# Other places in SBUF for the matmul operands of a two-layer encoder: weight buffers 32 bytes further apart each, x and three other tiles shifted

## The chip, the core and the metric

The kernel runs on one core of one Trainium2 chip. The metric is the device time of one execution in microseconds; the profile is one execution taken by the hardware profiler. SBUF is the on-chip memory that the engines work in: 128 partitions, and a tile lies at the same byte offset in each of them. "Place" below means that offset. TensorE (PE) multiplies a stationary operand of 128 columns (the weight load, PEld) with a moving operand that streams by, 256 or 512 columns here; both come from SBUF, and the sum goes to PSUM, in banks of 512 fp32 columns.

## The reference

A sequence of 512 positions by 1024 features passes two layers and a last norm. Layer 0 mixes positions by stick-breaking attention (16 heads of 64, causal), layer 1 by an RG-LRU block (projections, a causal convolution of four taps, gates per block, a linear recurrence). Each mixer is followed by an MLP of width 4096 with squared ReLU.

```python
def reference(x, ...):
    for layer in range(2):
        h = rms_norm(x, norm_mix[layer])
        y = stick_breaking_attention(h, w_qkv, w_o) if layer == 0 else rglru_block(h, ...)
        x = x + y
        h = rms_norm(x, norm_mlp[layer])
        x = x + jnp.square(jax.nn.relu(h @ mlp_w1[layer])) @ mlp_w2[layer]
    return rms_norm(x, norm_final)
```

All data are float32. The kernel keeps that precision with three products for one: each operand is split in a high half (rounded to the type fp32r, which TensorE takes in one pass) and a low half (the rest), and high by high, high by low and low by high are added up.

## The kernel before, in words

Features lie on partitions in 8 chunks of 128, positions along a partition. The normed x stands in `xgh` (high) and `xgl` (low), 8 chunks of 512 columns each; `bh` and `bl` (blocks, high and low) are of the same size and hold the mixer's output, and in an MLP the squared activations of its first half; `sh` and `sl` hold those of the second half.

Every weight tile of 128 by 1024 elements (4 KiB a partition) comes by DMA into a `raw` buffer (three of them). ScalarE (ACT) rounds it into `wh`, VectorE (DVE) writes the rest into `wl`, four buffers of each, and TensorE reads them. This goes round robin, so that each step's weights lie in the next of the four buffers. Where the layers need it, two further buffers of `wh` and `wl` stand in a pool of their own (`wmore`).

Three loops make nearly all of the matmuls:

- `dense` and `three` (L217 to L231): weights stationary, x or a block moving, 512 columns; for each of 8 chunks the triple `wh` by high, `wl` by high, `wh` by low. It does the q and k products, the output products of both mixers, the first quarter of the MLP, the RG-LRU projections.
- `v_steps` (L478 to L480): x stationary, weights moving, 256 columns.
- In the MLP a scheme with 7 products in place of 8 (blocks of a matrix are added ahead of the multiplication). `up` (L966) multiplies with weights stationary and 256 columns moving: chunks of `xgh` and `xgl`, or sums of chunks, whose high halves stand in `s41` (and in the last chunk of `bh`, `bl`) and whose low halves stand in eight tiles `low`. `times` (L1061) has the activations stationary (`bh`, `bl`, `sh`, `sl`) and the weights moving, 512 columns.

TensorE's order is written out by the code (it is scheduled by hand); in the MLP and the RG-LRU part the order on ACT and DVE is fixed too (class `Ordered`, the string `ORDER`). PE takes one instruction after the other; weights for the next matmul are loaded beside the one that runs.

The places follow from the order in which the pools and tiles are opened. Tiles of one pool stand one behind the other and each begins at a multiple of 32 bytes. In the kernel before nearly all operands are whole numbers of 512 bytes long, and everything that lies between them is a few small tiles. So all four buffers of `wh` and of `wl` begin at the same offset in a 512-byte grid. The table gives the places as the built program has them, taken modulo 512, in the two kernels:

| operand | before | after |
|---|---|---|
| `xgh`, `xgl` in attention and the RG-LRU part | 32 | 128 |
| `xgh`, `xgl` in both MLPs | 32 | 256 |
| `bh`, `bl` | 32 | 256 |
| the four `wh`, and `wl` of the same step | 288, 288, 288, 288 | 256, 288, 320, 352 |
| two more `wh`, `wl` in the RG-LRU part | 480 | 96 |
| `sh`, `sl` (second half of the activations) | 480 in layer 0, 96 in layer 1 | 128 |
| `s41` | 480 in layer 0, 96 in layer 1 | 96 |
| `low`, 8 tiles | 480 (one of them 96 in layer 1) | 96 |
| q, k, v halves, transposed weights of attention | 480 | 96 |

A chunk of x is 2048 bytes and a column block of weights 512, so a chunk's or block's own place in the 512-byte grid is that of its tile.

Of the kernel before, what the change touches and what calls it, by code (L numbers as in the profile page):

```python
# [24 lines left out]
EPS = 1e-6  # L25
RG_C = 8.0
SCALE = HD ** -0.5


START = [  # L30
# [31 lines left out]
def hybrid_encoder(  # L62
# [55 lines left out]
    V.memset(eps_t, EPS)  # L118
# [22 lines left out]
    class Squares:  # L141


        def __init__(self):
            self.acc = work.tile([P, S], F32, tag="ssq", name="ssq", bufs=1)
            self.begun = False
# [16 lines left out]
        def inv_squares(self, ps):  # L163

            for t in range(S // P):
                PE.matmul(
                    ps[:, t : t + 1], self.acc[:, t * P : (t + 1) * P], ones[:, 0:1],
                    start=True, stop=True,
                )
            n = S // P  # L170
            rr = work.tile([P, 2 * n], F32, tag="rr", name="rr", bufs=1)
            V.tensor_scalar(rr[:, :n], ps[:, :n], 1.0 / D, EPS, ALU.mult, ALU.add)
            V.reciprocal(rr[:, :n], rr[:, :n])
            V.tensor_scalar(rr[:, n:], rr[:, :n], -1.0, None, ALU.mult)
            return rr


    def slab_parts(src, cuts):

        raw = wpool.tile([P, C, P], F32, tag="raw", name="raw", bufs=3)  # L180
        wh = wpool.tile([P, C, P], F32R, tag="wh", name="wh")
        wl = wpool.tile([P, C, P], F32R, tag="wl", name="wl")
# [12 lines left out]

        return wh, wl, fetch, part
# [5 lines left out]
    def slab(src, cut=1, ks=range(C)):  # L202
        raws = rawpools[next(loads) % len(rawpools)]
        raw = raws.tile([P, C, P], F32, tag="raw", name="raw", bufs=3 if raws is wpool else 1)
        k = slice(ks.start, ks.stop)
        nc.sync.dma_start(out=raw[:, k, :], in_=src[:, k, :])
        pool = wpools[next(slabs) % len(wpools)]
        wh = pool.tile([P, C, P], F32R, tag="wh", name="wh")
        wl = pool.tile([P, C, P], F32R, tag="wl", name="wl")
        for i in range(cut):  # L210
            k = slice(ks.start + i * len(ks) // cut, ks.start + (i + 1) * len(ks) // cut)
            A.copy(wh[:, k, :], raw[:, k, :])  # L212
# [18 lines left out]
    def beside(ws, ah, al, pss, at, ks=range(C)):  # L231
# [7 lines left out]

    ctx.enter_context(tc.manual_schedule(engines={mybir.EngineType.PE}))  # L240


    lams = {
        n: const.tile([P, C], F32, tag=f"lam_{n}", name=n)
        for n in ("ab", "pp", "den", "s1", "s2", "pl", "c8", "c4")
    }
    c8, c4 = lams["c8"], lams["c4"]

    def softplus():

# [28 lines left out]
    NB = S // P  # L279
    PAIRS = H // 2  # L280
    half = [slice(0, HD), slice(HD, P)]
    so, early = {}, {}
# [7 lines left out]
    with ExitStack() as actx:  # L290
        hp = actx.enter_context(tc.tile_pool(name="hp", bufs=2))
        sp = actx.enter_context(tc.tile_pool(name="sp", bufs=1))


        later = sp.tile([P, S], F32, tag="later", name="later")
        G.memset(later, 0.0)
        G.affine_select(
# [11 lines left out]
        for i in range(2):  # L309
            both = []  # L310
            for nm in ("h", "l"):
                t = sp.tile([P, 2 * P], F32R, tag=f"last{nm}{i}", name=f"last{nm}{i}")
                G.memset(f(t[:, :P]), 0.0)
                both.append(t)
            lasts.append(both)
# [117 lines left out]
        def inverse():  # L433
# [333 lines left out]
    class Mlp:  # L767
# [28 lines left out]
        def __init__(self, ctx, layer):  # L796
            self.layer, self.sq, self.first = layer, Squares(), None
            self.V, self.A = Ordered(V), Ordered(A)
            self.mp = ctx.enter_context(tc.tile_pool(name=f"mlp{layer}", bufs=2))
            self.c = [  # L800
                self.mp.tile([P, 2, S], F32, tag=f"c{i}", name=f"c{i}", bufs=1) for i in range(4)
            ]
            self.begun, self.a = set(), {}
            self.turns = count()
            self.blocks = ExitStack()
            self.bp = self.blocks.enter_context(tc.tile_pool(name=f"blocks{layer}", bufs=2))
            self.u, self.lows, self.s3, self.slots = {}, {}, [], None

            self.s41 = self.bp.tile([P, C // 2, S], F32R, tag="s41", name="s41", bufs=1)

        def y(self, t, h):

# [207 lines left out]

        def operand(self, raw):
            pool = wpools[next(slabs) % len(wpools)]
            wh = pool.tile([P, C, P], F32R, tag="wh", name="wh")
            wl = pool.tile([P, C, P], F32R, tag="wl", name="wl")
# [288 lines left out]
    with ExitStack() as mctx:  # L1313
        mlp = Mlp(mctx, 0)
# [4 lines left out]
        last = {}  # L1319
# [57 lines left out]
    with ExitStack() as rctx:  # L1377
# [48 lines left out]

        def weights_high(key):
            pool = wmore if next(made) % 6 > 3 else wpool
            wh = pool.tile([P, C, P], F32R, tag="wh", name="wh")
            wl = pool.tile([P, C, P], F32R, tag="wl", name="wl")  # L1430
            ws[key] = wh, wl
            OA.copy(wh, raws[key])

# [140 lines left out]
        for k in range(C):  # L1574
            for c in range(4):
                ps, wh, wl = begun[c]
                three(ps, bh[:, k, :], bl[:, k, :], wh[:, k, :], wl[:, k, :], k == 0, k == C - 1)

    residual(w_ro, "mlp1", begun, {4: ws["o4"]})
    wctx.close()  # L1580


    with ExitStack() as mctx:
        lp = mctx.enter_context(tc.tile_pool(name="last", bufs=1))
        mlp = Mlp(mctx, 1)

        def between(c):
# [20 lines left out]
                )  # L1608


        A.activation(lp.tile([P, 1], F32, tag="rt", name="early"), eps_t, AF.Sqrt)

        ss = lp.tile([P, NB, 3], F32, tag="ss", name="ss")
        bias = lp.tile([P, NB], F32, tag="bias", name="bias")

        def square(t, h, i, cols=slice(0, S), end=False):

# [129 lines left out]
```

## Time and profile before

| | |
|---|---|
| median of 2 runs | 1048.83 us (1048.66 to 1049.0) |
| the profiled execution, span from the first to the last instruction | 1047.9 us |
| PE busy | 1035.1 us, 99% of the span, 5868 matmul records |
| DVE, ACT, POOL busy | 863.1, 701.5, 179.2 us |
| DMA | 159.41 MB, mean 152 GB/s |

The profile counts a span of 1047.9 us; the run's time is 0.9 us more than it. The end of a matmul is modelled in this profile, and matmuls are pipelined: one that is shown with 0.39 us starts 0.23 us ahead of the next. How long a matmul holds the engine is therefore read from the distance of two starts in the timeline, not from its own duration. For that a stretch is taken in which nothing but matmuls of one kind follow each other: the start of the last minus the start of the first, by the number between.

### The profile page before, as it was taken

Reading aid. Unit: us, or ns where it says so; the run is one execution under the profiler, and the core shown is the slowest. Engines: PE = TensorE matmul, PEld = TensorE weight load, DVE = VectorE, ACT = ScalarE, POOL = GpSimd, SP = SyncE. Lnnn points to the kernel's source line nnn. Section 1 sums busy time; section 2 is a strip of 40 time slices with the busy share of each in tenths; the row PEclk is TensorE's granted clock in tenths of the full one; section 3 lists DMA queues with packets and bytes.
Section 4 is the critical chain, followed back from the end, with each engine's and each line's share of the span. In section 5 each row is a group of like instructions: output and inputs, shape, how many; then the busy total and the mean of one; then the engine's idle time right before and its main releaser. Section 6 shows DMA issues by size and latency. Waiting matters only on the chain.

```text
span 1047.9 us, 15859 instructions
## 1 busy us (share of the span) xinstructions
PE 1035.1 (99%) x5868; PEld 902.8 (86%) x5868; DVE 863.1 (82%) x1147; ACT 701.5 (67%) x1082; POOL 179.2 (17%) x238
## 2 busy tenths in 40 slices
PE   8999999999999999999999999999999999999997
PEld 7888888888888988988988788888888988988986
DVE  7888787848788898898899799984789797897897
ACT  6767676836766773773775699964755773773775
POOL 2344344420000010010011121200000010010013
PEclk9999999999999999999999999999999999999999
DMA  6745354537536667567582483352345667567553
GB/s 225 204 137 141 101 149 104 153 109 274 149 80 190 181 139 204 165 140 207 164 208 81 109 214 112 91 221 93 88 86 173 174 142 206 158 139 204 145 125 101
DMA packets 52828, 159.41 MB, mean 152 GB/s; under 512 B 6672, under 2 KB 7952, under 8 KB 52752
## 3 DMA queue, kind: packets, MB, share of 16 engines
q1 hardware_dynamic: 41808, 120.13, 34.4%
q0 software_dynamic: 10368, 37.75, 20.9%
q8 instruction: 46, 0.75, 0.3%
q10 hardware_dynamic: 576, 0.52, 0.2%
q14 instruction: 30, 0.25, 0.1%
HBM read 137.41 MB, written 4.19 MB: 135 GB/s over the span
## 4 chain that ended last, share of the span: by engine, by line
PE 88%; DVE 5%; ACT 3%; issue 2%; DMA 2%; ACTq 0%; POOL 0%; DVEq 0%; POOLq 0%
PE ps_t L1061 14%; PE ps_acc L966 8%; PE ps_z L966 8%; PE ps_acc L1061 7%; PE ps_acc L219 5%; PE ps_acc L221 5%; PE ps_acc L220 5%; PE ps_o L966 5%; PE ps_z L1061 4%; PE ps_o L219 2%; PE ps_t L220 2%; PE ps_o L220 2%; PE ps_o L221 2%; PE ps_t L221 2%; PE ps_t L219 2%
## 5 line engine op out<-in xcount | busy, mean ns | idle before, releaser
L757 ACT CAST wh<-b 128x1024 fp32r<-128x1024 f32 x168 | 174.0, 1047 | 125.6 <-DVE b L757 76.7
L757 DVE TENSOR_TENSOR wl<-b,wh 128x1024 fp32r<-128x1024 f32 x168 | 203.8, 1221 | 50.5 <-ACT wh L757 50.1
L1043 POOL DMA_DIRECT2D b<-in_w_dn x40 | 35.0, 875 | 360.9 <-DVE b L757 204.6
L219 PE MATMUL ps_acc<-xgh,wh 128*128 128x512 f32 x192 | 78.5, 409 | 0.0
L221 PE MATMUL ps_acc<-xgl,wh 128*128 128x512 f32 x192 | 75.2, 392 | 0.0
L220 PE MATMUL ps_acc<-xgh,wl 128*128 128x512 f32 x192 | 75.1, 391 | 0.0
L581 DVE TENSOR_TENSOR_SCAN scan<-keep,later 128x128 f32<-128x128 f32 (+1 forms) x64 | 59.6, 933 | 18.8 <-ACT keep L571 10.9
L214 DVE TENSOR_TENSOR wl<-raw,wh 128x512 fp32r<-128x512 f32 (+2 forms) x70 | 60.9, 895 | 16.2 <-ACT wh L212 16.1
L757 ACT ACTIVATE u<-u 128x512 f32<-128x512 f32 x100 | 63.1, 632 | 6.5 <-DVE u L757 4.8
L212 ACT CAST wh<-raw 128x512 fp32r<-128x512 f32 (+2 forms) x70 | 50.8, 759 | 23.1 <-PE ps_acc L221 7.3
L1043 POOL DMA_DIRECT2D b<-in_w_up x24 | 20.8, 867 | 240.5 <-DVE b L757 72.1
L585 POOL TENSOR_TENSOR w<-w,scan 128x128 f32<-128x128 f32 (+1 forms) x64 | 51.9, 813 | 55.9 <-DVE scan L581 53.2
L757 DVE TENSOR_TENSOR b<-b,b 128x1024 f32<-128x1024 f32 x48 | 58.7, 1224 | 1.3
L757 DVE TENSOR_TENSOR u<-u 128x512 f32<-128x512 f32 (+1 forms) x92 | 54.9, 596 | 2.7 <-ACT u L757 1.1
L966 PE MATMUL ps_z<-xgh,wh 128*128 128x256 f32 x192 | 54.2, 282 | 0.0
L966 PE MATMUL ps_z<-xgh,wl 128*128 128x256 f32 x192 | 54.1, 282 | 0.0
L757 ACT CAST wh<-raw 128x1024 fp32r<-128x1024 f32 x46 | 47.9, 1045 | 9.3 <-PE ps_acc L1061 8.4
L966 PE MATMUL ps_acc<-low,wh 128*128 128x256 f32 x192 | 53.6, 279 | 0.0
L1061 PE MATMUL ps_t<-wl,sh 128*128 128x512 f32 x126 | 50.1, 398 | 0.0
L1061 PE MATMUL ps_t<-wh,sh 128*128 128x512 f32 x126 | 49.6, 394 | 0.0
L1061 PE MATMUL ps_t<-wh,sl 128*128 128x512 f32 x126 | 49.4, 392 | 0.0
L1061 PE MATMUL ps_t<-wh,bh 128*128 128x512 f32 x126 | 49.2, 391 | 0.0
(399 smaller groups left out, 3434.4 us busy)
## 6 DMA issues: line engine op xcount, KB each, us to landing
b<-in_w_dn SPq DMA_DIRECT2D x48, 512.0 KB, 4.5
b<-in_w_dn POOLq DMA_DIRECT2D x40, 512.0 KB, 5.5
b<-in_w_up SPq DMA_DIRECT2D x36, 512.0 KB, 4.6
b<-in_w_up POOLq DMA_DIRECT2D x24, 512.0 KB, 5.3
raw<-in_w_m SPq DMA_DIRECT2D x16, 512.0 KB, 4.1
raw<-in_w_dn SPq DMA_DIRECT2D x16, 512.0 KB, 4.7
raw<-in_w_in SPq DMA_DIRECT2D x16, 512.0 KB, 4.2
raw<-in_w_qk SPq DMA_DIRECT2D x12, 512.0 KB, 3.7
```

Source lines behind the costliest of these rows:

```text
L212: A.copy(wh[:, k, :], raw[:, k, :])
L214: V.tensor_tensor(wl[:, k, :], raw[:, k, :], f(wh[:, k, :]), ALU.subtract)
L219: PE.matmul(ps, wh, ah, start=start, stop=False)
L220: PE.matmul(ps, wl, ah, start=False, stop=False)
L221: PE.matmul(ps, wh, al, start=False, stop=stop)
L581: V.tensor_tensor_scan(sc[:, S - n : S][:, ::-1], keep[:, :n][:, ::-1], later[:, S - n :][:, ::-1], 1.0, ALU.mult, ALU.max,)
L585: G.tensor_tensor(wt, wt, sc[:, S - n + 1 : S + 1], ALU.mult)
L757: ins = getattr(self.e, name)(*args, **kwargs)
L966: PE.matmul(ps[:, i * HS : (i + 1) * HS], m, y, start=new and i == k == n == 0, stop=i == 1 and k == C // 2 - 1 and n == 2, skip_group_che ...
L1043: G.dma_start(out=unit[b].rearrange("p j n -> p (j n)"), in_=unit["src"](to), accum_op=ALU.add)
L1061: PE.matmul(ps, m, y[:, jj, cols], start=first and n == 0, stop=last and n == 2, skip_group_check=not new,)
```

## The change

Nothing is computed otherwise. The instructions of every engine stand in the same order as before, with the same shapes; one of them (a one-column square root that loads ACT's table early, at the start of the second MLP) writes into an unused column of another tile. What changes are the places:

- `wh` and `wl` come from pools of their own, each buffer 8 elements (32 bytes) longer than its data; `colt` (the columns of scales, 384 bytes) lies between the two pools, so that `wh` and `wl` of one step lie at the same offset in the 512-byte grid.
- `xgh` and `xgl` have 32 elements (128 bytes) of room more. `x_at` says at which end of it x lies: at 0 in attention and in the RG-LRU part, 128 bytes further in both MLPs.
- `s41` is 32 bytes longer, so that `sh` and `sl` and the raw blocks behind it move by 32 bytes against it; small tiles (`lams`, `ss`, `bias`, the `last` tiles) are opened elsewhere, and `rr` is 64 bytes in place of 32.

```diff
+ASIDE = 32
+APART = 8
+STEP = 8
+LINE = 16
...
     wpool = ctx.enter_context(tc.tile_pool(name="wpool", bufs=4))
+    halfpools = {}
+    halfpools["wh"] = ctx.enter_context(tc.tile_pool(name="whpool", bufs=4))
+    mid = ctx.enter_context(tc.tile_pool(name="mid", bufs=1))
+    halfpools["wl"] = ctx.enter_context(tc.tile_pool(name="wlpool", bufs=4))
...
-    colt = const.tile([P, cols.shape[1]], F32, tag="colt", name="colt")
+    colt = mid.tile([P, cols.shape[1]], F32, tag="colt", name="colt")
...
-    xgh = const.tile([P, C, S], F32R, tag="xgh", name="xgh")
-    xgl = const.tile([P, C, S], F32R, tag="xgl", name="xgl")
+    xgh_t = const.tile([P, C * S + ASIDE], F32R, tag="xgh", name="xgh")
...
+    xgl_t = const.tile([P, C * S + ASIDE], F32R, tag="xgl", name="xgl")
+    xgh = xgl = None
+
+    def x_at(aside):
+
+        nonlocal xgh, xgl
+        xgh, xgl = (
+            t[:, aside : aside + C * S].rearrange("p (c s) -> p c s", s=S) for t in (xgh_t, xgl_t)
+        )
+
+    x_at(0)
...
-            rr = work.tile([P, 2 * n], F32, tag="rr", name="rr", bufs=1)
+            rr = work.tile([P, LINE], F32, tag="rr", name="rr", bufs=1)
...
+    def weights(pool, tag):
+
+        step = STEP * (pool is wpool)
+        pool = halfpools[tag] if step else pool
+        t = pool.tile([P, C * P + step], F32R, tag=tag, name=tag)
+        return t[:, : C * P].rearrange("p (k f) -> p k f", f=P)
...
-        wh = pool.tile([P, C, P], F32R, tag="wh", name="wh")
-        wl = pool.tile([P, C, P], F32R, tag="wl", name="wl")
+        wh = weights(pool, "wh")
+        wl = weights(pool, "wl")
...
+    x_at(ASIDE)
     residual(w_so, "mlp0", so, so_next)
...
-            self.s41 = self.bp.tile([P, C // 2, S], F32R, tag="s41", name="s41", bufs=1)
+            t = self.bp.tile([P, C // 2 * S + APART], F32R, tag="s41", name="s41", bufs=1)
+            self.s41 = t[:, : C // 2 * S].rearrange("p (k s) -> p k s", s=S)
...
         def end(ws, xs):
+            x_at(0)
             for i in range(2):
...
+    x_at(ASIDE)
     residual(w_ro, "mlp1", begun, {4: ws["o4"]})
...
-        lp = mctx.enter_context(tc.tile_pool(name="last", bufs=1))
         mlp = Mlp(mctx, 1)
...
-        A.activation(lp.tile([P, 1], F32, tag="rt", name="early"), eps_t, AF.Sqrt)
+        A.activation(mlp.c[0][:, 0, :1], eps_t, AF.Sqrt)
```

More of the change, by code (lines that the diff above doesn't have):

```diff
@@ L116, in hybrid_encoder @@
     make_identity(nc, ident)
+    xgh_t = const.tile([P, C * S + ASIDE], F32R, tag="xgh", name="xgh")
     eps_t = const.tile([P, 1], F32, tag="eps", name="eps_t")
     V.memset(eps_t, EPS)
-    xgh = const.tile([P, C, S], F32R, tag="xgh", name="xgh")
-    xgl = const.tile([P, C, S], F32R, tag="xgl", name="xgl")
+    bias = const.tile([P, S // P], F32, tag="bias", name="bias")
+    ss = const.tile([P, S // P, 3], F32, tag="ss", name="ss")
+    lams = {
+        n: const.tile([P, C], F32, tag=f"lam_{n}", name=n)
+        for n in ("ab", "pp", "den", "s1", "s2", "pl", "c8", "c4")
+    }
+    c8, c4 = lams["c8"], lams["c4"]
+    xgl_t = const.tile([P, C * S + ASIDE], F32R, tag="xgl", name="xgl")
[6 more added lines that the diff above has]
+    x_at(0)
     bh = const.tile([P, C, S], F32R, tag="bh", name="bh")
@@ L170, in inv_squares @@
             n = S // P
-            rr = work.tile([P, 2 * n], F32, tag="rr", name="rr", bufs=1)
+            rr = work.tile([P, LINE], F32, tag="rr", name="rr", bufs=1)
             V.tensor_scalar(rr[:, :n], ps[:, :n], 1.0 / D, EPS, ALU.mult, ALU.add)
             V.reciprocal(rr[:, :n], rr[:, :n])
-            V.tensor_scalar(rr[:, n:], rr[:, :n], -1.0, None, ALU.mult)
+            V.tensor_scalar(rr[:, n : 2 * n], rr[:, :n], -1.0, None, ALU.mult)
             return rr
+    def weights(pool, tag):
[3 more added lines that the diff above has]
+        return t[:, : C * P].rearrange("p (k f) -> p k f", f=P)
     def slab_parts(src, cuts):
         raw = wpool.tile([P, C, P], F32, tag="raw", name="raw", bufs=3)
-        wh = wpool.tile([P, C, P], F32R, tag="wh", name="wh")
-        wl = wpool.tile([P, C, P], F32R, tag="wl", name="wl")
+        wh = weights(wpool, "wh")
+        wl = weights(wpool, "wl")
         def fetch(i, queue=nc.sync):
@@ L240, in hybrid_encoder @@
     ctx.enter_context(tc.manual_schedule(engines={mybir.EngineType.PE}))
[L243 to L247, printed above, removed]
     def softplus():
@@ L292, in hybrid_encoder @@
         sp = actx.enter_context(tc.tile_pool(name="sp", bufs=1))
+        last_of = {
+            (nm, i): sp.tile([P, 2 * P], F32R, tag=f"last{nm}{i}", name=f"last{nm}{i}")
+            for i in range(2) for nm in "hl"
+        }
         later = sp.tile([P, S], F32, tag="later", name="later")
@@ L311, in hybrid_encoder @@
             for nm in ("h", "l"):
-                t = sp.tile([P, 2 * P], F32R, tag=f"last{nm}{i}", name=f"last{nm}{i}")
+                t = last_of[nm, i]
                 G.memset(f(t[:, :P]), 0.0)
@@ L1022, in operand @@
             pool = wpools[next(slabs) % len(wpools)]
-            wh = pool.tile([P, C, P], F32R, tag="wh", name="wh")
-            wl = pool.tile([P, C, P], F32R, tag="wl", name="wl")
+            wh = weights(pool, "wh")
+            wl = weights(pool, "wl")
             wh, wl = (t.rearrange("p (j k) f -> p j (k f)", j=2) for t in (wh, wl))
@@ L1428, in weights_high @@
             pool = wmore if next(made) % 6 > 3 else wpool
-            wh = pool.tile([P, C, P], F32R, tag="wh", name="wh")
-            wl = pool.tile([P, C, P], F32R, tag="wl", name="wl")
+            wh = weights(pool, "wh")
+            wl = weights(pool, "wl")
             ws[key] = wh, wl
@@ L1608, in factors @@
                 )
-        A.activation(lp.tile([P, 1], F32, tag="rt", name="early"), eps_t, AF.Sqrt)
-        ss = lp.tile([P, NB, 3], F32, tag="ss", name="ss")
-        bias = lp.tile([P, NB], F32, tag="bias", name="bias")
+        A.activation(mlp.c[0][:, 0, :1], eps_t, AF.Sqrt)
         def square(t, h, i, cols=slice(0, S), end=False):
```

## The prediction

> **What bounds the kernel now.** I read the page first, then who waits on PE, then busy time by stage, then the timeline of PE in stretches of one kind. The page:
>
> ```profile
> span 1047.9 us, 15859 instructions
> PE 1035.1 (99%) x5868; PEld 902.8 (86%) x5868; DVE 863.1 (82%) x1147; ACT 701.5 (67%) x1082; POOL 179.2 (17%) x238
> ...
> PEclk9999999999999999999999999999999999999999
> ...
> PE 88%; DVE 5%; ACT 3%; issue 2%; DMA 2%; ACTq 0%; POOL 0%; DVEq 0%; POOLq 0%
> ```
>
> PE is busy in 99% of the span, at a granted clock of 0.9 or more in every slice, and holds 88% of the chain that ended last. A busy PE need not be a PE at its peak, so the next question is whether it waits. The view of waits on PE, longest first:
>
> ```profile
> PE ps_z L437 <- DVE ssq L422: 1.6, 1, 1.6
> PE ps_z L381 <- DVE eps_t L118: 1.1, 1, 1.1
> PE ps_z L966 <- ACT u L757: 1.0, 1, 1.0
> PE ps_t L220 <- DVE wl L757: 0.8, 1, 0.8
> ```
>
> These are the four longest, 4.5 us of 1047.9 together. No engine and no DMA can give more than that back. What is left is the pace of the matmuls themselves. The busy time by stage, for one MLP stretch of each layer, says who would be next:
>
> ```profile
> core 0: us, PE busy (x) PEld busy (x) DVE busy (x) ACT busy (x) POOL busy (x), PEclk, DMA share, GB/s
> 290.00:460.00 170.00, 170.00 (x1071) 153.39 (x1071) 147.41 (x193) 116.37 (x153) 16.50 (x19) 1.00 0.63 160
> 764.00:920.00 156.00, 154.97 (x984) 139.74 (x983) 134.98 (x152) 99.23 (x127) 13.89 (x16) 1.00 0.62 162
> ```
>
> DVE has 147.41 of 170 us (87%) and 134.98 of 156 us (87%). A PE that is 2 to 4% faster still does not catch up with DVE's sum. The pace of PE, in the timeline: of each stretch the first row and the row that follows its last.
>
> ```profile
> 439.53 0.28 PE L966 MATMUL ps_o<-s,wh 128*128 128x256 f32 x1
> ...
> 442.25 0.28 PE L966 MATMUL ps_z<-xgh,wh 128*128 128x256 f32 x1
> ...
> 447.94 0.28 PE L966 MATMUL ps_z<-xgh,wh 128*128 128x256 f32 x1
> ...
> 450.82 0.40 PE L1061 MATMUL ps_t<-wh,bh 128*128 128x512 f32 x1
> ...
> 805.67 0.28 PE L966 MATMUL ps_acc<-s,wh 128*128 128x256 f32 x1
> ...
> 808.50 0.39 PE L966 MATMUL ps_acc<-bh,wh 128*128 128x256 f32 x1
> ```
>
> Each of the three stretches is one half product of `up`: 24 matmuls of the same shape, no wait between. The first takes 2.72 us, 113.3 ns each; it streams `s41` and `low` of layer 0, which lie at 480 in the 512-byte grid, past weights at 288. The second takes 2.88 us, 120.0 ns each; it streams x, at 32, past the same weights. The third is the first one's product in layer 1, where `s41` and one `low` lie at 96: 2.83 us, 117.9 ns. Only places differ. With 512 columns:
>
> ```profile
> 294.86 0.39 PE L1061 MATMUL ps_t<-wh,bh 128*128 128x512 f32 x1
> ...
> 300.30 0.39 PE L1061 MATMUL ps_t<-wh,sh 128*128 128x512 f32 x1
> ...
> 302.82 0.39 PE L1061 MATMUL ps_t<-wh,sl 128*128 128x512 f32 x1
> ...
> 769.24 0.40 PE L1061 MATMUL ps_t<-wh,sh 128*128 128x512 f32 x1
> ...
> 772.04 0.40 PE L1061 MATMUL ps_z<-wh,bh 128*128 128x512 f32 x1
> ```
>
> From 294.86 to 300.30 lie 24 matmuls with `bh` and `bl` (at 32) stationary: 226.7 ns each. From 300.30 to 302.82 are 11 with `sh`, `sl` at 480: 229.1 ns. From 769.24 to 772.04 are 12 with the same tiles at 96, in layer 1: 233.3 ns. So the place of an operand is worth up to 6.7 ns in a matmul, and PE does some 5,500 of these one after the other: that is what bounds the kernel and what the change touches.
>
> The numbers have a grain. 120.0 - 113.3 and 233.3 - 226.7 are both 6.7 ns; 226.7 - 120.0 = 106.7 ns for 256 columns more is 0.417 ns a column, so 6.7 ns are 16 columns, 64 bytes of fp32. In such steps the stretches are 17, 18, 34 and 35 long, while the columns alone would make 16 and 32. In the kernel before nearly every moving tile begins at 32, 96, 288 or 480, that is 32 bytes past a multiple of 64: a row of 2048 bytes then touches 33 pieces of 64 bytes and not 32. I take one of the surplus steps to be that piece. This reading is mine; no row shows the cause.
>
> The Trainium skill, in "SBUF — State Buffer", section "Who interferes with whom", has TensorE read moving operand and weights through two ports of its own, and says that it never waits on anyone; by that rule no place matters and the sum is the time before, 1048.8 us. The trace disagrees: the same 24 matmuls took 2.72 and 2.88 us.
>
> **The change, part by part.** The order on all engines is the same, so nothing is moved past anything, no wait is added, and no DMA is issued elsewhere. The 32 bytes more in a buffer are never read. The early square root has no reader; it runs on ACT while PE is busy, as before, at no cost as long as PE does not wait for ACT. What is left is the pace, by kinds. Counts are summed from the view of groups by form, of which the largest are:
>
> ```profile
> L219 PE MATMUL ps_acc<-xgh,wh 128*128 128x512 f32 x192 | 78.5, 409 | 0.0
> L966 PE MATMUL ps_z<-xgh,wh 128*128 128x256 f32 x192 | 54.2, 282 | 0.0
> L1061 PE MATMUL ps_t<-wl,sh 128*128 128x512 f32 x126 | 50.1, 398 | 0.0
> ```
>
> Moving x or blocks, 512 columns: 1,488 in L219 to L221, 48 in L427, 48 in the gates, 1,584 in all. After the change these tiles lie at 128 or 256, on a multiple of 64. At one step less each: 1,584 x 6.67 ns = 10.6 us.
>
> Moving weights, 512 columns (L1061): 1,332. Two of the four buffers lie at 256 and 320, on a multiple of 64, two at 288 and 352, past it. By the program 652 of them begin on one: 652 x 6.67 = 4.3 us. The others stay as they are.
>
> 256 columns: in `up` 1,248 of 2,016 will begin on a multiple of 64 (x, and the parts of `bh`, `bl`), and in `v_steps` 192 of 384. Here the row of 120.0 ns falls by a step to that of 113.3: 1,440 x 6.67 = 9.6 us. The other 768 of `up` (`s41`, `low`, at 96) I leave where they are: they have 113.3 in layer 0 and 117.9 in layer 1, with room for a gain or a loss of a step, 5.1 us either way, which goes to the range.
>
> Sum: 10.6 + 4.3 + 9.6 = 24.5 us. The profiled execution has a span of 1047.9 us and 0.9 us around it, and so stands at the median, 1048.8: 1048.8 - 24.5 = **1024.3 us**.
>
> Against this stand two rows. The first is, apart from transposes and sums with `ones`, the only moving stream of the kernel before that begins on a multiple of 64 (`lasth`, `lastl` at 64), and a like one beside it:
>
> ```profile
> 190.01 0.28 PE L629 MATMUL ps_o<-th,v 128*128 128x256 f32 x1
> ...
> 190.25 0.28 PE L478 MATMUL ps_acc<-wh,xgh 128*128 128x256 f32 x1
> ...
> 190.97 0.28 PE L629 MATMUL ps_o<-lasth,v 128*128 128x256 f32 x1
> ...
> 191.20 0.28 PE L478 MATMUL ps_acc<-wh,xgh 128*128 128x256 f32 x1
> ```
>
> Two matmuls in 0.24 us past a boundary, two in 0.23 us on it: a step less in both would have been 0.013 us. This neither shows nor excludes the gain, since both pairs stand alone between others. So a gain of nothing is the other bound of these 24.5 us. The second row is on what happens when the relation between moving and stationary tile changes:
>
> ```profile
> 289.83 0.40 PE L221 MATMUL ps_o<-xgl,wh 128*128 128x512 f32 x1
> ...
> 292.14 0.39 PE L219 MATMUL ps_o<-xgh,wh 128*128 128x512 f32 x1
> ...
> L757 ACT CAST wh<-b 128x1024 fp32r<-128x1024 f32 x168 | 174.0, 1047 | 125.6 <-DVE b L757 76.7
> ...
> L212 ACT CAST wh<-raw 128x512 fp32r<-128x512 f32 (+2 forms) x70 | 50.8, 759 | 23.1 <-PE ps_acc L221 7.3
> ...
> L757 ACT CAST wh<-raw 128x1024 fp32r<-128x1024 f32 x46 | 47.9, 1045 | 9.3 <-PE ps_acc L1061 8.4
> ```
>
> Ten matmuls right after other work took 2.31 us, 231 ns each, before the stretch settled to 226.7: 43 ns lost. Now the four buffers lie alike, and a new step's weights change nothing; after the change every step's weights lie 32 bytes off the last one's. The casts into `wh` count up to 168 + 70 + 46 = 284 steps: 284 x 0.043 = 12.2 us if each has to settle anew, nothing if the pace follows at once. I take nothing for the forecast, since the stretch at 300.30 went over to its pace (229.1) within its first matmuls, and keep 12.2 us for the range.
>
> **The rivals.** (1) The places change nothing on balance: the 64-byte grain is there, but the surplus steps have nothing to do with where a stream begins, and relations that gain a step and relations that lose one cancel. For it: `lasth` above; against it: 113.3 and 120.0 ns. 1048.8 us. (2) As (1), with each step settling anew: 1048.8 + 12.2 = 1061.0 us. For it: 289.83 to 292.14; against it: weights that go to another place at 300.30 without such a stretch. (3) Slower: what counts is the distance of the two streams in the 512-byte grid, and the new distances are the bad ones. Many of the pairs of places in the new table occur nowhere in the trace of before. If all 2,916 matmuls of 512 columns (1,584 + 1,332) come to the row of 233.3 from 226.7 and the 768 of `up` from 113.3 to 120.0, that is 19.4 + 5.1 = 24.5 us, 1073.3 us; beyond 2% (21 us) it takes 86% of it. Against it: 233.3 is the worst settled pace of the trace, and part of the kernel has it already. (4) PE gets faster, and DVE or ACT becomes the wait. At 87% of the stretch DVE could bind only in places; this takes a part of the gain, not its sign, and belongs to the spread of the forecast.
>
> **How the numbers follow.** The forecast, a step less for streams on a boundary: chance 0.62, 1024.3 us, its own range 1012 (the other 768 of `up` and the 680 weights past a boundary gain a step as well, 5.1 + 4.5 us, and the 666 of L1061 with `sh`, `sl` come from 231 ns, the mean of 229.1 and 233.3, to 226.7, 3.0 us) to 1037 (half of the 24.5 us does not come). Rival 1: 0.15, rival 2: 0.12, rival 3: 0.11. The range reaches from 1010 us to 1060 us: it leaves out rival 3 and the ends of the forecast and of rival 2. About 2%, 21 us, is what a measurement of this kernel can tell from no change. Faster by more (below 1027.9): 0.44, the larger part of the forecast's own range. Slower by more (above 1069.8): 0.08, from rival 3. Within: 0.48, of which 0.18 are the forecast's upper end, 0.27 rivals 1 and 2, 0.03 rival 3.
>
> **What the profile after would show.** The forecast is right if a stretch of 24 matmuls of `up` that streams x takes 2.72 us and no longer 2.88, if `dense` goes from 226.7 to 220 ns, and if L1061 has two paces, one for each second buffer. If `dense` stays at 226.7 and the time falls nevertheless, the gain came from distances and not from the boundary. Rival 2 would show as a slow first third of each product, rival 3 as whole stretches at 233. If the waits on PE sum up to more than 5 us, rival 4 has a part. The forecast is wrong above all if the piece of 64 bytes that a stream touches in excess costs nothing.

## The result, and the profile after

The kernel after takes 1057.43 us (median of 2 runs, 1057.15 to 1057.7), the kernel before 1048.83 us. The ratio is 1.0079, with a 95% interval from 1.0049 to 1.0108: 0.8% slower, less than the 2% that a measurement of this kernel is taken to tell from no change, but away from zero. The forecast of 1024.3 us had the wrong sign; the time lies inside the range on record.

The page after, with the rows that answer to those of before:

```profile
span 1055.3 us, 15859 instructions
PE 1042.7 (99%) x5868; PEld 902.7 (86%) x5868; DVE 864.0 (82%) x1147; ACT 702.2 (67%) x1082; POOL 180.2 (17%) x238
...
PEclk9999999999999999999999999999999999999999
...
PE 92%; DVE 2%; ACT 2%; DMA 2%; issue 2%; ACTq 0%; POOL 0%; SPq 0%; DVEq 0%; POOLq 0%
```

The span is 7.4 us longer (1055.3 against 1047.9), PE's busy time 7.6 us (1042.7 against 1035.1), at the same granted clock and with the same number of matmuls. The busy times of DVE and ACT have hardly changed (863.1 and 701.5 us before), and PE's share of the chain went up from 88% to 92%. PE's own busy time is thus longer by as much as the span: the extra time is not waiting, the matmuls themselves go slower. Where, the timeline of PE shows. First `dense` in the first MLP, where 24 matmuls lie between each row and the next. Before:

```profile
261.04 0.39 PE L221 MATMUL ps_o<-xgl,wh 128*128 128x512 f32 x1
...
266.48 0.39 PE L221 MATMUL ps_t<-xgl,wh 128*128 128x512 f32 x1
...
271.92 0.39 PE L221 MATMUL ps_t<-xgl,wh 128*128 128x512 f32 x1
```

The same places of the program after:

```profile
262.83 0.39 PE L252 MATMUL ps_o<-xgl,wh 128*128 128x512 f32 x1
...
268.42 0.40 PE L252 MATMUL ps_t<-xgl,wh 128*128 128x512 f32 x1
...
273.87 0.39 PE L252 MATMUL ps_t<-xgl,wh 128*128 128x512 f32 x1
...
279.49 0.40 PE L252 MATMUL ps_acc<-xgl,wh 128*128 128x512 f32 x1
...
285.09 0.39 PE L252 MATMUL ps_acc<-xgl,wh 128*128 128x512 f32 x1
```

Before, every 24 take 5.44 us, 226.7 ns each. After, they take 5.59, 5.45, 5.62 and 5.60 us: 233, 227, 234 and 233 ns. x lies at 256 throughout, the weights of the four stretches at 288, 256, 352 and 320. Only the stretch whose weights lie at x's own place keeps the pace of before; the three buffers that the change moved off it cost 0.15 to 0.18 us a stretch. And x at 256, a multiple of 64, is no faster than x at 32 was (5.45 against 5.44 us).

Then three half products of `up` with x, 24 matmuls each, after:

```profile
350.70 0.28 PE L998 MATMUL ps_z<-xgh,wh 128*128 128x256 f32 x1
...
353.43 0.28 PE L998 MATMUL ps_acc<-xgh,wh 128*128 128x256 f32 x1
...
356.31 0.28 PE L998 MATMUL ps_z<-xgh,wh 128*128 128x256 f32 x1
...
359.13 0.28 PE L998 MATMUL ps_o<-s,wh 128*128 128x256 f32 x1
```

They take 2.73, 2.88 and 2.82 us, with weights at 320, 256 and 352. The middle one has x and weights at one place, as all such stretches had before, and takes what they took (2.88 us).

I call *distance* the start of the moving operand minus that of the stationary operand loaded for the next matmul, modulo 256 bytes (inside a stretch that is also the distance to the matmul's own stationary operand, since all of a step's weights lie alike). The two sets of rows then read: with 512 columns, distance 0 gives 227 ns and 224, 160, 192 give 233 to 234; with 256 columns, distance 0 gives 120.0 ns, 192 gives 114 and 160 gives 117.5. For each kind of matmul I added up the time from its start to the next start in the profiled executions. In the first seven rows, a matmul whose successor starts over 245 ns (512 columns) or 130 ns (256) later is counted at 230 or 118 ns, and what is over is put down as a stall; before has 14.6 us of such stalls, 8.1 of them in `dense` of attention, where the first 30 us have a granted clock of 0.94. The sums are `s41` and `low`. Differences to before in us; the other columns are the experiments below:

| kind (matmuls) | after | 3 | 4 | 5 | 6 | 7 | 8 |
|---|---|---|---|---|---|---|---|
| `dense` after attention (1,029) | +4.9 | 0.0 | +4.1 | +2.6 | +2.3 | +1.3 | 0.0 |
| `times`, `bh` and `bl` (678) | +2.6 | +0.1 | +2.5 | +0.7 | -0.5 | -0.3 | -0.5 |
| `times`, `sh` and `sl` (677) | +1.2 | -0.1 | +0.3 | +1.2 | -2.7 | -2.5 | -2.7 |
| `up` with x (1,056) | -1.5 | 0.0 | -1.6 | +0.1 | -2.2 | -4.4 | 0.0 |
| `up` with `s41`, `low` (768) | +1.3 | 0.0 | +1.6 | +2.3 | +0.9 | -0.5 | -0.9 |
| `up` with `bh`, `bl` (192) | +0.2 | 0.0 | +0.1 | 0.0 | 0.0 | 0.0 | 0.0 |
| products of attention (843) | +0.1 | +0.1 | +0.7 | +0.2 | +0.1 | +0.1 | +0.1 |
| stalls | -2.3 | -0.7 | -1.5 | -1.9 | +2.9 | +5.5 | +1.5 |
| all others | +0.8 | -0.5 | -0.7 | -0.1 | -1.2 | +0.1 | -0.5 |
| sum | +7.3 | -1.0 | +5.4 | +5.2 | -0.6 | -0.8 | -3.2 |

Each column is one execution of each kernel, and its sum lies 0.3 to 2.3 us below the difference of the medians given with the experiments (for after 7.3 against 8.6 us). After loses 8.7 us in matmuls of 512 columns outside attention (4.9 + 2.6 + 1.2), gains 1.5 us in `up` with x and loses nearly as much with the sums. Its stalls are 2.3 us less. Of this, 1.0 us lies in `times`, where a slower PE can wait less; 1.6 us lies in `dense`, and there experiment 3 has 1.4 us less as well, at the paces of before, so that part is not an effect of the slower PE.

The Trainium skill, "SBUF — State Buffer", section "Who interferes with whom", gives TensorE one read port for the moving operand and an independent one for the weights, and says that it never waits on anyone. If that holds between its own two reads too, the places could not have cost anything; the stretches of 5.44 and 5.60 us disagree.

### The profile page after: what moved, and what is told of

Read it like the earlier page. It is cut to its first block, busy times and chain, and to the rows that moved or that the text cites. A ratio compares the mean times of both kernels' runs of the same rounds, so it can differ in the third digit from the quotient of the medians.

```text
span 1055.3 us, 15859 instructions
## 1 busy us (share of the span) xinstructions
PE 1042.7 (99%) x5868; PEld 902.7 (86%) x5868; DVE 864.0 (82%) x1147; ACT 702.2 (67%) x1082; POOL 180.2 (17%) x238
## 4 chain that ended last, share of the span: by engine, by line
PE 92%; DVE 2%; ACT 2%; DMA 2%; issue 2%; ACTq 0%; POOL 0%; SPq 0%; DVEq 0%; POOLq 0%
PE ps_t L1093 15%; PE ps_acc L1093 8%; PE ps_acc L998 8%; PE ps_z L998 8%; PE ps_acc L250 5%; PE ps_acc L251 5%; PE ps_acc L252 5%; PE ps_o L998 5%; PE ps_z L1093 4%; PE ps_t L250 2%; PE ps_t L251 2%; PE ps_t L252 2%; PE ps_o L250 2%; PE ps_o L251 2%; PE ps_o L252 2%; PE ps_t L633 2%
## 5 line engine op out<-in xcount | busy, mean ns | idle before, releaser
L788 ACT CAST wh<-raw 128x1024 fp32r<-128x1024 f32 x46 | 47.9, 1045 | 9.2 <-PE ps_acc L1093 8.6
```

The source lines that it names most:

```text
L788: ins = getattr(self.e, name)(*args, **kwargs)
```

## The experiments

The theory: the pace of a matmul depends on its distance, and not on where its stream begins. Its rivals: the boundary of 64 bytes (the forecast on record), settling anew at each change of place (rival 2), and, once matmuls get faster, a wait for DVE or ACT (rival 4).

### Experiment 1: the distance by itself

A kernel of its own, with nothing but these matmuls:

```diff
+    def run(ps, n, m, w, count):
+        m, w = m // 4, w // 4
+        for i in range(count):
+            a = m + i % 2 * S
+            b = w + i % 8 * P
+            PE.matmul(ps[:, :n], st[:, b : b + P], mv[:, a : a + n],
+                start=i == 0, stop=i == count - 1)
...
+    for n, m, w in GROUPS:
+        run(ps[7], n, m, w, 24)
+        run(ps[next(turn) % 7], n, m, w, 48)
```

> Leaves out the whole computation: one tile of moving and one of stationary data, groups of 24 and then 48 matmuls whose places are shifted against each other in steps of 16 bytes, with 512 and with 256 columns moving; nothing else runs meanwhile, and the output means nothing. Three theories. (D) The pace hangs on the distance d from the start of the weights to the start of the moving operand, taken modulo 256 bytes, and on nothing else: with 512 columns 226.7 ns at d = 0, 229 at 64, 232.5 to 234.5 at 32, 96, 128, 160, 192 and 224; with 256 columns 113.3 at 192, 117 at 32, 118 at 64 and 224, 120 at 0 and 96; the same at d + 256, and the same when both operands are shifted by 32 or 64 bytes together. (B) The pace hangs on the start of the moving operand alone: with 512 columns about 6.7 ns less at a moving start on a multiple of 64 bytes than 32 bytes past one, whatever d is, and both shifted by 32 at d = 0 costs 6.7 ns more than both unshifted. (S) Each change of place has to settle: where the weights go from one place to another every 24 matmuls, the 192 matmuls of such a pattern take some 43 ns more per change than those whose weights stay; with places 256 bytes apart (D) expects no difference from weights that stay, and with 0, 32, 64, 96 bytes the mean of the single distances, about 232 ns for 512 columns against 226.7.

Rows of its timeline, one for 48 matmuls. The moving operand stands at 0, 32, 64, 192 and 256 bytes from the weights; in the sixth row both are shifted by 32; then, with 256 columns, at 0, 192 and 16:

```profile
19.47 11.04 PE L73 MATMUL psa<-mv,st 128*128 128x512 f32 x48
...
35.95 11.36 PE L73 MATMUL psb<-mv,st 128*128 128x512 f32 x48
...
52.66 11.15 PE L73 MATMUL psc<-mv,st 128*128 128x512 f32 x48
...
119.72 11.36 PE L73 MATMUL psg<-mv,st 128*128 128x512 f32 x48
...
153.18 11.04 PE L73 MATMUL psb<-mv,st 128*128 128x512 f32 x48
...
420.54 11.04 PE L73 MATMUL psd<-mv,st 128*128 128x512 f32 x48
...
517.22 5.92 PE L73 MATMUL psc<-mv,st 128*128 128x256 f32 x48
...
568.39 5.82 PE L73 MATMUL psb<-mv,st 128*128 128x256 f32 x48
...
653.50 5.60 PE L73 MATMUL pse<-mv,st 128*128 128x256 f32 x48
```

A row is 47 starts and one matmul of 0.39 or 0.28 us, so (11.04 - 0.39) / 47 = 226.6 ns, and 233.4, 228.9 for 11.36, 11.15; with 256 columns 120.0, 117.9 and 113.2 ns. Distance 256 is like 0, and shifting both by 32 or by 64 changes nothing. The moving operand at 32 is slow past weights at 0 and fast past weights at 32: the boundary theory is refuted, and the matmuls waited for no other engine. One expected pace failed: 256 columns at 192 took 117.9 ns here and not 113.3, though the same distance gave 113.3 ns in the last part of the probe; experiment 2 takes this up.

For settling, the weights changed place every 24 matmuls. The start of each group of 24, weights at 0, 32, 64, 96 and 0 again, 512 columns:

```profile
872.96 5.61 PE L73 MATMUL psg<-mv,st 128*128 128x512 f32 x24
878.41 5.75 PE L73 MATMUL psa<-mv,st 128*128 128x512 f32 x24
884.00 5.76 PE L73 MATMUL psb<-mv,st 128*128 128x512 f32 x24
889.60 5.77 PE L73 MATMUL psc<-mv,st 128*128 128x512 f32 x24
895.21 5.65 PE L73 MATMUL psd<-mv,st 128*128 128x512 f32 x24
900.70 5.75 PE L73 MATMUL pse<-mv,st 128*128 128x512 f32 x24
```

From start to start they take 5.45, 5.59, 5.60, 5.61 and, back at 0, 5.49 us; with weights that stay, or that go to and fro by 256 bytes, all take 5.44. So a return to distance 0 costs 0.05 us, near the 43 ns of the prediction (in after's own timeline it is 0.01 us, 5.45 against 5.44), and the other changes of place cost nothing beyond the new pace itself.

### Experiment 2: what ran before, and how fine the distance is

```diff
+    for (n, d), (n2, d2) in ENTRIES:
+        run(ps[7], n, d, 0, 24)
+        run(ps[next(turn) % 7], n2, d2, 0, 48)
```

> Leaves out the whole computation, as the first probe, and the output means nothing. First part: distances of 4, 8, 12, 20, 24 and 28 bytes. If the grain is 16 bytes, 4 to 12 are like 0 (226.7 ns with 512 columns, 120.0 with 256) and 20 to 28 like 16 (231.7 and 113.3); if the grain is the element, each differs. Second part: groups of 48 matmuls, each entered from 24 of another distance or width. If the pace is a function of distance and width alone, all groups of one distance and width have one pace, whatever came before; if it also keeps a phase from what ran before, 256 columns at 192 have two, 113.3 and 117.8 ns, since the first probe showed both. Third part: the weights go to and fro between two places (32 bytes apart with 512 columns; 128 apart; 16 apart with 256 columns), and the moving operand stands either where the weights of its own matmul stand, or where those of the next matmul stand, which are loaded while it streams. If the load beside the stream is what counts, 512 columns take 226.7 ns in the second case and about 233 in the first; if a matmul's own weights count, it is the other way round.

The shown loop is the second part: each group of 48 is entered from 24 matmuls of another distance or width. The rows: 512 columns at 4 and 20 bytes; 256 columns at 112, entered from 512 columns at 0 and from 256 at 0; 256 columns at 192, entered from the same two:

```profile
19.60 11.52 PE L69 MATMUL psa<-mv,st 128*128 128x512 f32 x48
...
69.96 11.68 PE L69 MATMUL psd<-mv,st 128*128 128x512 f32 x48
...
363.11 5.64 PE L69 MATMUL pse<-mv,st 128*128 128x256 f32 x48
...
382.46 5.66 PE L69 MATMUL psg<-mv,st 128*128 128x256 f32 x48
...
410.01 5.82 PE L69 MATMUL psc<-mv,st 128*128 128x256 f32 x48
...
429.70 5.62 PE L69 MATMUL pse<-mv,st 128*128 128x256 f32 x48
```

The grain is finer than 16 bytes: 236.8 ns at 4 and 240.2 at 20, worse than any multiple of 16. And distance is not all. At 192 (the last two rows) the pace stays at 117.9 ns after one entry and comes to 113.3 after the other; at 112 it came to 113.3 in its second half from all five entries that were tried. The third part told nothing apart: with weights that go to and fro by 32 and the moving operand beside its own weights the pace was 233.4 ns, beside the next ones 231.7, and by 128 it was 228.4 and 230.0. Neither came to 226.7, so which of the neighbouring loads counts stays open. What ran before may also reach far back: in experiments 2 and 9, 256 columns at 8 bytes came after the same 96 matmuls (at 4 and at 8 bytes), and in the program only what lay before those differed:

```profile
126.63 5.76 PE L69 MATMUL psa<-mv,st 128*128 128x256 f32 x48
...
833.53 6.24 PE L58 MATMUL psa<-mv,st 128*128 128x256 f32 x48
```

The first row is of experiment 2, 116.6 ns a matmul, the second of experiment 9, 126.8 ns. Each probe was profiled once, so what made them differ is not shown; a pace with 256 columns that was measured after one entry is therefore not yet the pace of that distance.

### Experiment 3: all operands on multiples of 64, distances kept

A tile of 32 bytes ahead of the operands moves all of them together (`lasth` and `lastl`, 32 matmuls, leave their multiple of 64 by it).

```diff
+    const.tile([P, 8], F32, tag="pad", name="pad")
     xgh = const.tile([P, C, S], F32R, tag="xgh", name="xgh")
```

> The kernel before with 32 bytes more ahead of all operands: every operand that began 32 bytes past a multiple of 64 begins on one, and all distances between operands are those of before. Forecast on record (a step of 6.7 ns less for each stream that begins on a multiple of 64): 24.5 us less than before or more, 1024 us. Distance theory: no change, 1048.8 us, ratio within 0.2% of 1. If changes of place have to settle: no change either, since nothing moves against anything else.

1048.97 us against 1049.65 for the kernel before beside it, ratio 0.9996 [0.9986, 1.0005]. The first two stretches of `up` that the prediction read, here with every operand on a multiple of 64:

```profile
440.18 0.28 PE L967 MATMUL ps_o<-s,wh 128*128 128x256 f32 x1
...
442.90 0.28 PE L967 MATMUL ps_z<-xgh,wh 128*128 128x256 f32 x1
...
448.59 0.28 PE L967 MATMUL ps_z<-xgh,wh 128*128 128x256 f32 x1
...
451.47 0.40 PE L1062 MATMUL ps_t<-wh,bh 128*128 128x512 f32 x1
```

2.72 and 2.88 us, as before. The gain of 24.5 us on record is not there.

### Experiment 4: the spread of the weights alone

A spacer behind the two weight pools keeps all other operands at their distances from the first buffer.

```diff
+    halfpools["wh"] = ctx.enter_context(tc.tile_pool(name="whpool", bufs=4))
+    mid = ctx.enter_context(tc.tile_pool(name="mid", bufs=1))
+    halfpools["wl"] = ctx.enter_context(tc.tile_pool(name="wlpool", bufs=4))
...
+        t = pool.tile([P, C * P + step], F32R, tag=tag, name=tag)
```

> The kernel before with one part of the change alone: the four buffers of the weights 32 bytes further apart each; x, blocks and all else stay at their places. Distance theory, worked out with the settled paces of the first probe: the sum of paces goes up by 8.4 us, with the mean paces of the two traces by 5.9 us: 1055 to 1057 us, most of what the whole change costs. Boundary theory (the forecast on record): the weights are on a multiple of 64 in two buffers of four, as in the kernel after, so L1061 gains 4.3 us and nothing else moves: 1044.5 us. Settling theory: up to 12.2 us more at the starts of products, with the settled part of each product unchanged.

1057.36 us against 1049.65, ratio 1.0063 [1.0051, 1.0076]. The column of experiment 4 in the table has 6.9 us of losses in `dense` and `times`, nearly those of after (8.7). The spread by itself costs nearly as much as the whole change, by moving three of four buffers off distance 0.

### Experiment 5: the kernel after without the spread

```diff
-STEP = 8
+STEP = 0
```

> The kernel after without the spread: all four buffers of the weights at 256 in the 512-byte grid (first buffer's place), everything else as after. Distances are then x 128 and bh 0 in attention, x 0 in the MLPs, bh 0, sh 128, sums 96. Distance theory with the mean paces of the two traces: the sum of paces is 4.8 us above that of before, 1053.5 us, so that the other places cost most of that and the spread the rest, though the spread alone cost 6.6 us: the two parts do not add up, since the spread averages over distances. Boundary theory: with all weights on a multiple of 64 a further gain of 4.5 us against the forecast on record, 1020 us. Settling theory: no change of place between steps any more, so before's 1048.8 us.

1055.15 us against 1049.34, ratio 1.0061 [1.0047, 1.0075]. `dense` in the first MLP, where x and all weights now lie at 256:

```profile
261.56 0.39 PE L252 MATMUL ps_o<-xgl,wh 128*128 128x512 f32 x1
...
267.00 0.39 PE L252 MATMUL ps_t<-xgl,wh 128*128 128x512 f32 x1
```

5.44 us again. What is left comes from the other places: `dense` (+2.6 us, most of it with x at distance 128 in the RG-LRU part), the sums at 96 (+2.3), `sh` and `sl` at 128 (+1.2). The spread alone costs 0.63%, the places alone 0.61%, both together 0.79%. The table shows where they do not add up: `dense` loses 4.1 and 2.6 us alone and 4.9 together, the sums 1.6 and 2.3 alone and 1.3 together. An operand that is off distance 0 already has less to lose by the spread, and may gain.

### Experiment 6: better distances, x at 192 in the MLPs

Before with x at distance 192 in both MLPs, `sh` and `sl` at 0 and the sums at 192 in both layers, without the spread.

```diff
+ROOM = 64
+ASIDE = 48
+APART = 16
...
+    xgh_t = const.tile([P, C * S + ROOM], F32R, tag="xgh", name="xgh")
...
+    x_at(ASIDE)
     residual(w_so, "mlp0", so, so_next)
...
+            t = self.bp.tile([P, C // 2 * S + APART], F32R, tag="s41", name="s41", bufs=1)
...
-        lp = mctx.enter_context(tc.tile_pool(name="last", bufs=1))
```

> The kernel before with other distances and no spread of the weights: in both MLPs x stands at 192 from the weights modulo 256 (0 before), the second half of the activations at 0 in both layers (64 and 192 before), the sums of blocks at 192 in both. Distance theory: the products of up with x go from 120.0 to 113.3 ns, or to 117.8 if they are entered badly (1,056 matmuls: 7.0 or 2.3 us less), the first quarter with x from 226.7 to 233.3 (376: 2.5 us more), L1061 with the second half from 228.9 and 233.3 to 226.7 (2.7 us less), the rest of up in layer 1 from 117.8 to 113.3 (1.0 us less): 8.2 us less in all, 1040.6 us, with the bad entry 1045.3. Boundary theory: x at 224 in the 512-byte grid is still past a multiple of 64, and so are all others, so no change: 1048.8 us. Settling theory: no change but for what the distances bring.

1050.67 us against 1049.65, ratio 1.0015 [1.0004, 1.0026]: no gain, if anything a small loss, where 1040.6 us or, with a bad entry, 1045.3 were expected. The stretch of `up` with x:

```profile
448.58 0.28 PE L983 MATMUL ps_z<-xgh,wh 128*128 128x256 f32 x1
...
451.41 0.39 PE L1078 MATMUL ps_t<-wh,bh 128*128 128x512 f32 x1
```

2.83 us, 117.9 ns: it is entered badly, as in experiment 2. `times` with `sh` and `sl` gained the 2.7 us expected, `up` with x 2.2, `dense` lost 2.3, and stalls took 2.9.

### Experiment 7: x at 112

```diff
-ASIDE = 48
+ASIDE = 28
```

> The same kernel as the one with x at 192 from the weights in the MLPs, but with x at 112. In the entry probe 256 columns at 192 went to 113.3 or stuck at 117.8 ns by what ran before, and at 112 went to 113.3 from each of five entries, after some ten matmuls (115.3 ns over the first 24). Distance theory with memory of the entry: x in up at 114 to 115 ns (119.4 before: 1,056 matmuls, 4.6 to 5.7 us less), the first quarter with x at 231.1 (1.7 us more), the second half of the activations at 226.7 as in the kernel with 192 (1.6 us less), the sums at 192 as there (2.5 us more, part of it waits for ACT at the start of a product): 3.0 to 4.1 us less than before, 1045 us. Distance alone, without memory: the same as with x at 192, 1050 us or less by 0.8 us. Boundary theory: no change, 1049 us.

1048.81 us against 1049.34, ratio 0.9994 [0.9985, 1.0002]. The same stretch:

```profile
449.68 0.28 PE L983 MATMUL ps_z<-xgh,wh 128*128 128x256 f32 x1
...
452.40 0.39 PE L1078 MATMUL ps_t<-wh,bh 128*128 128x512 f32 x1
```

2.72 us, 113.3 ns: the pace came as expected, and with it 6.4 us in all over the kinds of the table (1.3 - 0.3 - 2.5 - 4.4 - 0.5). The time did not: 1045 us were expected. The chain that ended last, and the view of waits on PE:

```profile
PE 72%; DVE 13%; ACT 7%; issue 4%; DMA 3%; ACTq 0%; POOL 0%; SPq 0%; DVEq 0%; POOLq 0%
```

```profile
PE ps_z L983 <- ACT u L773: 1.5, 1, 1.5
PE ps_t L1078 <- DVE wl L773: 1.3, 5, 0.3
...
PE ps_t L235 <- DVE wl L773: 0.8, 1, 0.8
```

PE's share of the chain falls from 88% to 72%, DVE's rises from 5% to 13% and ACT's from 3% to 7%. PE now comes to the joint between `up` and `times` five times before DVE has the low half of the weights ready (the row of L1078); the same view of before has no such row. With the weight loads counted in, the view of this line has, in before and in this kernel:

```profile
  DVE wl L757: 2.0, 6
...
  DVE wl L773: 7.4, 20
```

That is 2.0 us in 6 waits before and 7.4 us in 20 here, while DVE is busy as long as before (863.5 us). By the distances of starts, stalls took 5.5 us, of which 4.6 in `up` and `times`. This is rival 4, at some 6 us of gain.

### Experiment 8: x left at 0

```diff
-ASIDE = 48
+ASIDE = 0
```

> The kernel with x at 192 or 112, but with x at 0 from the weights as before: only the second half of the activations (to distance 0) and the sums in layer 1 (to 192) have moved. Distance theory: L1061 with the second half 1.6 us less; the sums in layer 1 (216 matmuls from 117.8 to 113.3) 1.0 us less if entered from x at 0 as in layer 0: 1046.2 us. If the 2.2 us that the sums' low parts took more in the kernel with x at 192 do not come from x: 1049 us or more.

1047.07 us against 1049.34, ratio 0.9985 [0.9976, 0.9994]: faster than before by 0.15%, near the 1046.2 us expected, but far below the 2% that count as a difference here. The stretch of `times` with `sh` in layer 1, 12 matmuls:

```profile
768.16 0.39 PE L1078 MATMUL ps_t<-wh,sh 128*128 128x512 f32 x1
...
770.88 0.39 PE L1078 MATMUL ps_z<-wh,bh 128*128 128x512 f32 x1
```

2.72 us against 2.80 in the kernel before (769.24 to 772.04 in the prediction): 226.7 and 233.3 ns, at distance 0 in place of 192. Of 4.1 us gained in paces (0.5, 2.7 and 0.9) stalls took 1.5 back.

### Experiment 9: is there a better distance?

```diff
+GROUPS = [(n, d, 0) for n in (512, 256) for d in range(4, 256, 4) if d % 16]
```

> Leaves out the whole computation, as the two probes before it, and the output means nothing. All distances from 4 to 252 bytes that are a multiple of 4 and not of 16, 24 and then 48 matmuls each, with 512 and with 256 columns. The question is whether the multiples of 16 measured so far hold the extremes. If the pace moves in whole steps of 16 columns that hang on 64-byte pieces, no distance is below 226.7 ns (512) or 113.3 ns (256). If it is a clash between two streams of reads, distances near 0 should be as bad as the 236.6 ns at 4 and the 240.0 ns at 20, and some distance could be below 226.7, down to 220 ns, which would be one step less; then a kernel with that distance would be worth building. My expectation: nothing below 226.7 and 113.3, the worst at 240 and 123.

The best row with 512 columns, at 60 bytes, and the worst with 256 columns, at 104:

```profile
204.31 11.12 PE L58 MATMUL pse<-mv,st 128*128 128x512 f32 x48
...
988.73 6.41 PE L58 MATMUL pse<-mv,st 128*128 128x256 f32 x48
```

228.3 and 130.4 ns (the worst expected was 123 with 256 columns; with 512 it is the 240 ns of 20 bytes again). None of the 48 distances with 512 columns is below 226.7 ns, and none with 256 below 113.3. With the 16 of experiment 1, distance 0 is the best of all 64 for 512 columns: the kernel before had most of its matmuls there, and there was little to win. With 256 columns each distance had one entry only, so a lower pace by another entry is not excluded.

## Why the prediction was wrong, point by point

**What bounds the kernel** was right: PE's pace, and places of the kernel before that are worth up to 6.7 ns a matmul. The waits are larger than the 4.5 us quoted: the view of waits counts from a matmul's modelled end, 0.39 us after its start, where the next is due after 0.23 us; by starts the stalls are 14.6 us, most of them ahead of the first MLP.

**The step that failed** is "I take one of the surplus steps to be that piece", the 64-byte piece that a stream 32 bytes past a boundary touches in excess. In the kernel before nearly every stream begins 32 bytes past a multiple of 64, so no row had a contrast in what I made the cause; the one exception (`lasth`) showed nothing. What did vary between the rows that I quoted was the distance: 192 in the stretch of 113.3 ns, 0 in that of 120.0, 64 in the `s41` two thirds of the one of 117.9 (its `low` stood at 480, at 192); with 512 columns 0 in 226.7, 64 in 229.1, 192 in 233.3. Experiment 3 shows the piece to be worth nothing (1048.97 against 1049.65 us), and experiment 1 the distance to be what counts. The grain of 6.7 ns that the piece was to explain was an accident of few rows: two of the six quoted paces (229.1 and 117.9 ns) did not fit it, and of the 48 paces of experiment 9 with 512 columns 44 lie on steps of 1.67 ns above 226.7, within 0.2 ns.

**The terms.** Moving x or blocks, -10.6 us: measured +4.9 in `dense` after attention and +0.4 in attention (the table's +0.1 there holds `v_steps` too). Moving weights in `times`, -4.3 us: measured +3.8 (2.6 + 1.2). 256 columns, -9.6 us: measured -1.5 in `up` with x, +0.2 with `bh` and `bl`, and -0.3 in `v_steps`, a gain, but one that comes from distances other than 0: the stretch of `up` whose x stood on a multiple of 64 at distance 0 kept its 2.88 us. The sums, from -5.1 to +5.1 us: +1.3. The waits, put at nothing: 2.3 us less, of which at most 1.0 can be told from the spread of single executions.

**Rival 2**, settling anew, 12.2 us: a return to distance 0 costs 0.05 us and other changes of place cost nothing, so of 284 steps only about a fourth can pay; 71 x 0.05 = 3.6 us is an upper estimate from experiment 1, a third of what I priced, and part of the sums above.

**Rival 3**, slower by distance, had the mechanism and the sign; I gave it 0.11. Its price of 24.5 us took every matmul of 512 columns to the bad pace and `up` from 113.3 to 120.0; in fact a fourth of the buffers stays at 0, `times` with `sh` was at a bad pace already, and `up` with x got better. My argument against it, that 233.3 ns is the worst settled pace and part of the kernel has it already, limits the loss and says nothing about its sign. With the known prices of distances 0, 64 and 192 put on the table of places, the sign of the loss in `dense` of the MLPs could have been suspected: three of four buffers leave the best of the three, one for 192 (233.3 ns), two for 160 and 224, which no row had.

**Rival 4** had no part in after, since PE became slower, but it met experiment 7 and in part 6: the 87% of DVE hid that it delivers just in time at the joints of `up` and `times`.

## What to carry to other kernels

Where matmuls of float32 halves run back to back, read their pace from the distances of starts, sort the stretches by the distance between moving operand and weights modulo 256 bytes, and keep that distance at 0 for 512 columns; 32 bytes of padding between weight buffers is enough to lose 3% on three of four. With 256 columns distance 0 was not the best, but the pace there hangs on what ran before as well, so it has to be measured in the kernel itself. A cause is worth a forecast only if the rows before hold both of its states; where they hold one, measure it alone first. And when a stage at 99% of one engine gets faster, ask at its joints, not over its mean, who delivers next: here 6 us of faster matmuls met 5.5 us of new stalls, 4.6 of them where `up` and `times` take their weights from engines that are busy for 87% or less.

## What the runs showed of the hardware

- With 512 columns the settled pace went from 226.7 ns (distance 0) to 240.2 (20 bytes), with 256 columns from 113.3 (16 and 112) to 130.4 (104). It repeated after 256 bytes and differed between neighbours 4 bytes apart (some 237 ns at 4, 232 at 8); a common shift of both operands by 32 or 64 bytes changed nothing. The Trainium skill, "TensorE: Matmul & The Clock Gate", section "Wait — 56ns, not 53.3ns?", gives 215.7 ns from start to start for 512 columns at the full clock, without a part of the places in it. No stretch of these fp32r matmuls came to it: the best was 226.7 ns, at a granted clock of 1.00 in that stage.
- Two settled paces can belong to one distance and width, by what ran before: 113.3 and 117.9 ns at 192 with 256 columns, 228.9 and 233.4 ns at 64 with 512. At 8 bytes with 256 columns two probes had 116.6 and 126.8 ns after the same 96 matmuls; what made them differ is not shown.
- That two streams of reads get in each other's way would fit this, but no run shows the cause: it is argued from the period and the distance, and which load counts was not settled.
